# Gate/up and down products of a two-layer trunk in three 256-column matmuls a k-step, with weight places that vary by output tile

## The chip, the cores and the metric

The kernel runs on one core of a Trainium2 chip. The metric is device time in microseconds of one launch. An engine is named as the profile names it: PE is TensorE (matmuls), PEld its weight loads, DVE is VectorE, ACT is ScalarE, POOL is GpSimd, SP the engine that issues most transfers.

## The reference

The reference is a decoder trunk of two layers on 256 tokens of width 2048, batch 1, in float32. Layer 0 mixes tokens by block-sparse attention (with 256 tokens there is one block, so it is causal attention over 16 heads of 128). Layer 1 uses multi-head latent attention: low-rank queries and keys/values of rank 512, and a shared rotary key. Each is followed by a gated feed-forward network of width 5632:

```
def conv_glu_ffn(h, w_gate, w_up, conv_w, conv_b, w_down):
    g = h @ w_gate
    g = causal depthwise conv of width 3 (g) + conv_b
    return (jax.nn.silu(g) * (h @ w_up)) @ w_down

for i in range(2):
    h = rms_norm(x, attn_norm[i])
    x = x + (moba_attention if i == 0 else mla_attention)(h, ...)
    h = rms_norm(x, ffn_norm[i])
    x = x + conv_glu_ffn(h, ...)
```

All weights are float32 and are used once, so each is read once from memory.

## The kernel before

**Two parts for each operand.** Every float32 operand of a large product is split into a high part and a low part, both of type float32r: the high part is a copy in that type, the low part the rest. A product is the sum of three: high by high, high by low and low by high. An activation tile holds, per block of 128 features, 256 columns of high parts (one per token) and then 256 of low parts. So a matmul of the high weights with 512 columns does two of the three products at once, in the two halves of a PSUM bank of 512 float32 numbers, and a matmul of the low weights with the first 256 columns does the third.

**The weight stream.** `Stream` (L48 to L112) brings the weights in 370 units of up to 1 MB. The host lays them out in the order of their use. A unit holds four pieces of 128 x 512. `load` (L70) issues the transfer on SP, three units ahead. `split` (L92) makes the parts of a piece: a copy on ScalarE for the high part (L103) and a subtraction on VectorE for the low one (L104), up to four pieces ahead of their use; five buffers of each part exist. Where a part begins in its buffer is set by `starts(u, j)` (L155): each buffer has 576 elements for 512, so a part can begin up to 64 elements in. Before the change, `starts` gives the feed-forward units and the latent query rank place 0, and multiples of 8 elements elsewhere: by group of four units in the query/key/value projections of layer 0 (`HEAD_STARTS`), by pair of output tiles in the two output projections (0, 8, ... 56), and by unit in the latent stage (`LATENT_STARTS`).

**The order of the work** is written out by hand. A quantum is one piece's matmuls; `at(q, f)` puts a step behind quantum q, `first` ahead of it. The loop at the end splits the parts ahead, issues the matmuls of the quantum, and then what hangs behind it, each on its engine's own queue.

**Three forms of matmul quanta.**
- `tok_major` (L236) has the tokens in the rows of the result. Its moving operand is the weights, 512 columns at a time (288 in one projection), three products for each of two token blocks (L246, L247, L248).
- `feat_major` (L250) has the features in the rows. Its stationary operand is a 128 x 128 square of the weights, and the pair described above is issued for each square: L272 with 512 columns, L274 with 256. It serves gate/up and down of both layers and the latent query rank.
- `feat_half` (L279) issues three products of 256 columns for each square, all into one half of a bank: high by high (L286), high by low (L287), low by high (L288). It serves the two output projections, and the last output tile of the last layer's down projection.

In `feat_major` and `feat_half` a piece holds four squares, which are four steps of the contraction for one output tile of 128 features. Gate and up have 44 output tiles each, with 16 such steps (one unit) a tile; down has 16 output tiles of 44 steps (11 pieces).

**Taking results out.** After a pair, the two halves of the bank must be summed. `halves` (L290) copies the second half with ScalarE into a tile (L293), adds a base if there is one (L295), and adds the first half with VectorE (L297). `evac_gate` (L711) uses it and then scales by the norm's factor; the causal conv, SiLU and scaling follow, one step a quantum. `product` (L735) uses it for the up projection and multiplies the gate by it; `high` and `low` then make the two parts of the activation tile `a`. `residual_halves` (L384) adds a down projection's output tile to the residual stream `xT`. `cq_part` uses it for the latent query rank. Four PSUM banks are there for accumulators.

**Stages of the span.** Query/key/value of layer 0 run up to about 303 us, its output projection to 399, gate/up to 888, down to 1132; the latent attention follows to 1292, its output projection to 1400, gate/up of layer 1 to 1889, and down to the end.

Of the kernel before, what the change touches and what calls it, by code (L numbers as in the profile page):

```python
# [14 lines left out]
ALU = mybir.AluOpType  # L15
PSUM = bass.MemoryType.PSUM

P = 128
S = 256
D = 2048  # L20
NT = S // P
KD = D // P
H = 16
DFF = 5632
NF = DFF // P
# [18 lines left out]
AHEAD_PIECES = 4  # L44
WO_OPEN = 8

UP_ORDER = ("pairs", "pairs")
DOWN_ORDER = ("pairs", "pairs")  # L48

ROOM = 64  # L50

HEAD_STARTS = (2, 1, 3, 2, 1, 3, 4, 5, 6, 7, 0, 2)
LATENT_STARTS = (1, 2, 3, 4, 5, 6, 7, 2, 2, 1, 1, 3, 3)

H_START = 8

# [58 lines left out]
def trunk(ctx: ExitStack, tc: tile.TileContext, a, out):  # L115
    nc = tc.nc
# [10 lines left out]
    mm = nc.tensor.matmul  # L127
# [26 lines left out]
    units += units_of("ffn_down1")  # L154
    def starts(u, j):  # L155

        step = 0
        if u < 48:
            step = HEAD_STARTS[u // 4]
        elif u < 64 or 222 <= u < 238:  # L160
            step = (u - 48) // 2 % 8 if u < 64 else (u - 222) // 2
        elif u == 200:
            step = 2
        elif 201 <= u < 209:
            step = u - 201
        elif 209 <= u < 222:
            step = LATENT_STARTS[u - 209]
        return 8 * step, 8 * step

    assert len(units) == 370  # L170
    ws = Stream(nc, raw_pool, part_pool, units, starts)


    att = ExitStack()
    att_pool = att.enter_context(tc.tile_pool(name="att", bufs=2))
    xT = keep.tile([P, KD, S], F32, name="xT")
# [49 lines left out]
    def at(q, f, *args):  # L226
        side.setdefault(q, []).append((f, args))

    def first(q, f, *args):
        ahead.setdefault(q, []).append((f, args))  # L230

    def add(f, *args):
        quanta.append((f, args))
        return len(quanta) - 1
# [12 lines left out]
            mm(o, hi, t_lo[:, :n], start=False, stop=False)  # L247
            mm(o, lo, t_hi[:, :n], start=False, stop=kt == k_last)  # L248

    def feat_major(state, rhs, k0, k_last, t_hi, t_lo, n, order="pairs"):  # L250

        if k0 == 0:
            state["acc"] = ps_acc.tile([P, 512], F32, name="acc")
        src, o = rhs(), state["acc"]
        ks = range(n // P)
        steps = {
            "pairs": [(k, part) for k in ks for part in "hl"],  # L260
            "low first": [(k, part) for k in ks for part in "lh"],
            "grouped": [(k, part) for part in "hl" for k in ks],
        }[order]
        for i, (k, part) in enumerate(steps):
            kt = k0 + k
            flags = dict(
                start=k0 == 0 and i == 0, stop=kt == k_last and i == len(steps) - 1,
                skip_group_check=True,
            )
            c = slice(k * P, (k + 1) * P)  # L270
            if part == "h":
                mm(o, t_hi[:, c], src[:, kt, :], **flags)  # L272
            else:
                mm(o[:, :S], t_lo[:, c], src[:, kt, :S], **flags)  # L274

    def open_half(state):
        state["acc"] = ps_acc.tile([P, 512], F32, name="acc")
# [1 line left out]
    def feat_half(state, rhs, k0, k_last, first, t_hi, t_lo, n, half):  # L279

        src = rhs()
        o = state["acc"][:, half * S : (half + 1) * S]
        for k in range(n // P):
            kt = k0 + k
            w_hi, w_lo = t_hi[:, k * P : (k + 1) * P], t_lo[:, k * P : (k + 1) * P]
            mm(o, w_hi, src[:, kt, :S], start=first and k == 0, stop=False, skip_group_check=True)  # L286
            mm(o, w_hi, src[:, kt, S:], start=False, stop=False, skip_group_check=True)  # L287
            mm(o, w_lo, src[:, kt, :S], start=False, stop=kt == k_last, skip_group_check=True)  # L288

    def halves(dst, acc, base=None):  # L290

        t = small.tile([P, S], F32, name="half", bufs=2)
        nc.scalar.copy(t, acc[:, S:])  # L293
        if base is not None:
            nc.vector.tensor_tensor(t, t, base, op=ALU.add)  # L295
        dst = t if dst is None else dst
        nc.vector.tensor_tensor(dst, acc[:, :S], t, op=ALU.add)  # L297
        return dst
# [82 lines left out]
            xT[:, j, :], xT[:, j, :], state["acc"][:, half * S : (half + 1) * S], op=ALU.add  # L381
        )

    def residual_halves(state, j):  # L384
        halves(xT[:, j, :], state["acc"], xT[:, j, :])

    def store(j):
        nc.sync.dma_start(out[:, j, :], xT[:, j, :])
# [227 lines left out]
    for g in range(4):  # L616
        for kind in "qkv":
            state = {}
            for kt in range(KD):
                q = add(tok_major, state, lambda: n1.h, kt, KD - 1)  # L620
# [67 lines left out]
    ffn = {}  # L688
# [13 lines left out]
    class FTile:  # L702
# [7 lines left out]

        def evac_gate(self):  # L711
            self.g = ffn["g"][self.j % 2]
            halves(self.g[:, 2:], self.gate["acc"])
            nc.vector.tensor_tensor(self.g[:, 2:], self.g[:, 2:], self.norm.rstd_b, op=ALU.mult)

        def conv_last(self):
            self.c = ffn["pool"].tile([P, S], F32, name="c")
# [15 lines left out]
            nc.vector.tensor_tensor(self.c, self.c, self.norm.rstd_b, op=ALU.mult)  # L733

        def product(self):  # L735
            u = halves(None, self.up["acc"])
            nc.vector.tensor_tensor(self.c, self.c, u, op=ALU.mult)

        def high(self):
# [8 lines left out]
    def plan_gate_up(layer, norm):  # L748
        for j in range(NF):
            f = FTile(layer, j, norm)  # L750
            for kind, st in (("g", f.gate), ("u", f.up)):
                for kq in range(4):
                    q = add(lambda t_hi, t_lo, n, st=st, kq=kq: feat_major(
                        st, lambda: norm.h, 4 * kq, KD - 1, t_hi, t_lo, n, UP_ORDER[layer]))
                if kind == "g":
                    if j == 0:
                        at(q, open_ffn, layer)
                    at(q, f.evac_gate)
                    at(q + 1, f.conv_last)
                    at(q + 2, f.conv_rest)  # L760
                    at(q + 3, f.silu)
                    at(q + 4, f.scaled)
                else:
                    at(q, f.product)
                    at(q + 1, f.high)
                    at(q + 2, f.low)

    plan_gate_up(0, n2)

    n3 = Norm(C_AN + KD, False)  # L770

    def plan_down_feat(norm, layer):
        for j in range(KD):
            st = {}
            tail = norm is None and j == KD - 1
            if tail:
                first(len(quanta), open_half, st)
            for kq in range(NF // 4):
                if tail:
                    q = add(lambda t_hi, t_lo, n, st=st, kq=kq: feat_half(  # L780
                        st, lambda: ffn["a"], 4 * kq, NF - 1, kq == 0, t_hi, t_lo, n, 0))
                else:
                    q = add(lambda t_hi, t_lo, n, st=st, kq=kq: feat_major(
                        st, lambda: ffn["a"], 4 * kq, NF - 1, t_hi, t_lo, n, DOWN_ORDER[layer]))
            if tail:
                at(q, residual, st, j, 0)
            else:
                at(q, residual_halves, st, j)
            if norm is None:
                at(q, store, j)  # L790
            elif j < KD - 1:
                norm.plan(q + 2, j)
            else:
                at(q, norm.now, j)
                at(q + 3, norm.sums)
        return q

    plan_down_feat(n3, 0)


# [116 lines left out]
    for r in range(4):  # L917
        state = {}
        for kq in range(4):
            q = add(lambda t_hi, t_lo, n, st=state, kq=kq: feat_major(  # L920
                st, lambda: n3.h, 4 * kq, KD - 1, t_hi, t_lo, n))
            if r == 0 and kq == 0:
                at(q, open_mla)
        at(q, cq_part, state, r)
# [45 lines left out]
    for half in range(2):  # L970
        state = {}
        for kt in range(KD):
            q = add(tok_major, state, lambda: n3.h, kt, KD - 1)
# [22 lines left out]
    for g in range(4):  # L996
        if g == 1:
            rotary_queries(1, 2)
        for kind in "kqv" if g else "qkv":
            state = {}  # L1000
            for kt in range(4):
                q = add(tok_major, state, lambda kind=kind: env["cqT" if kind == "q" else "ckvT"], kt, 3)
# [18 lines left out]
    n4 = Norm(C_FN + KD, True)  # L1021
    plan_wo(n4, WO_ORDER2)
    plan_gate_up(1, n4)

    plan_down_feat(None, 1)


# [122 lines left out]
```

## Time and profile before

| | us |
|---|---|
| two runs | 2138.54 and 2138.88, median 2138.71 |
| the profiled execution | 2138.94 |
| its span, first to last instruction | 2137.1 |
| gate/up of layer 0, layer 1 | 399 to 888, 1400 to 1889 |
| down of layer 0, layer 1 | 888 to 1132, 1889 to the end |

A row of a group gives its line, engine, operation, the tile written and those read, the shape and the count; behind the first bar the busy time and the mean duration in ns of one; behind the second the engine's idle time just before it and what ended it. A row of a window gives, after its bounds, its length, and for PE, PEld, DVE, ACT and POOL the busy time and the count of instructions, then the granted clock as a share of full speed, the share of the transfer engines that was busy, and GB/s. Matmuls overlap in the rows, because the next one streams in while the last one drains, so the pace is read from starts or from counts over a window, not from durations. A row of the timeline gives the start in us and the duration.

### The profile page before, as it was taken

To read this page: it belongs to the slowest core of one execution; us is meant where nothing else is said; L and a number is where in the kernel's file an instruction comes from. 1 tells how busy PE (TensorE), PEld (TensorE's weight loads), DVE (VectorE), ACT (ScalarE), POOL (GpSimd) and SP (SyncE) were. 2 spreads that over 40 slices of the span, in tenths; PEclk is the share of its full clock that TensorE was granted. 3 is DMA by queue.
4 is the path that set the end of the run, shared out by engine and by line. 5 is a ranking of instruction groups with operands and counts; after the bars stand their busy time and mean duration, and the time that the engine had idled before them with its cause. 6 is when DMAs were issued, how large, how long until landed. Compare 5 with 4: busy or idle time off the path is not lost.

```text
span 2137.1 us, 33882 instructions
## 1 busy us (share of the span) xinstructions
PE 2129.4 (100%) x12439; PEld 1883.5 (88%) x12439; DVE 1461.7 (68%) x3246; ACT 1184.6 (55%) x2418; POOL 45.6 (2%) x37
## 2 busy tenths in 40 slices
PE   9999999999999999999999999999999999999999
PEld 7888889988888888888889889998888888888888
DVE  6766666777777777755556786777777777765554
ACT  6555555555555555545455675555555555554443
POOL 0000000000000000000000110000000000000000
PEclk9999999999999999999999999999999999999999
DMA  7444445455555555555554433555555555555553
GB/s 268 160 175 178 158 158 191 176 186 197 184 191 196 182 194 192 187 195 185 198 188 156 177 132 119 178 178 197 182 193 194 182 196 189 186 202 205 189 203 129
DMA packets 59350, 391.30 MB, mean 183 GB/s; under 512 B 6960, under 2 KB 10032, under 8 KB 13232
## 3 DMA queue, kind: packets, MB, share of 16 engines
q1 hardware_dynamic: 59040, 389.10, 51.6%
q8 instruction: 98, 1.61, 0.3%
q14 instruction: 68, 0.56, 0.1%
q10 hardware_dynamic: 144, 0.04, 0.0%
HBM read 387.01 MB, written 2.10 MB: 182 GB/s over the span
## 4 chain that ended last, share of the span: by engine, by line
PE 97%; DVE 1%; DMA 0%; issue 0%; ACT 0%; POOL 0%; SPq 0%; POOLq 0%; ACTq 0%; DVEq 0%
PE acc L272 45%; PE acc L274 24%; PE acc L247 5%; PE acc L248 5%; PE acc L246 5%; PE acc L286 3%; PE acc L288 3%; PE acc L287 3%; PE sc L511 1%; PE tp L487 1%; PE sc L558 1%; PE tp L547 0%; PE sc L514 0%; DVE wlo L104 0%; PE sc L559 0%; DMA xT<-in_xT 0%
## 5 line engine op out<-in xcount | busy, mean ns | idle before, releaser
L104 DVE TENSOR_TENSOR wlo<-raw,whi 128x512 fp32r<-128x512 f32 (+1 forms) x1480 | 991.1, 683 | 385.9 <-ACT whi L103 382.5
L103 ACT CAST whi<-raw 128x512 fp32r<-128x512 f32 (+1 forms) x1480 | 866.4, 614 | 280.3 <-PE acc L272 173.9
L272 PE MATMUL acc<-h,whi 128*128 128x512 f32 x2880 | 999.2, 390 | 0.0
L274 PE MATMUL acc<-h,wlo 128*128 128x256 f32 x2880 | 812.1, 282 | 0.0
L272 PEld LDWEIGHTS acc<-h,whi 128*128 128x128 f32 x2880 | 540.6, 188 | 113.1
L274 PEld LDWEIGHTS acc<-h,wlo 128*128 128x128 f32 x2880 | 544.3, 189 | 0.0
L272 PE MATMUL acc<-a,whi 128*128 128x512 f32 x1364 | 472.9, 390 | 0.0
L274 PE MATMUL acc<-a,wlo 128*128 128x256 f32 x1364 | 384.6, 282 | 0.0
L272 PEld LDWEIGHTS acc<-a,whi 128*128 128x128 f32 x1364 | 256.0, 188 | 53.7
L274 PEld LDWEIGHTS acc<-a,wlo 128*128 128x128 f32 x1364 | 257.8, 189 | 0.0
L293 ACT COPY half<-acc 128x256 f32<-128x256 f32 x211 | 78.7, 373 | 308.3 <-PE acc L274 308.1
L246 PE MATMUL acc<-whi,h 128*128 128x512 f32 (+1 forms) x448 | 177.1, 395 | 0.0
L247 PE MATMUL acc<-wlo,h 128*128 128x512 f32 (+1 forms) x448 | 171.0, 382 | 0.5 <-DVE wlo L104 0.5
L248 PE MATMUL acc<-whi,h 128*128 128x512 f32 (+1 forms) x448 | 170.1, 380 | 0.0
L286 PE MATMUL acc<-oT,whi 128*128 128x256 f32 x512 | 146.9, 287 | 0.0
L288 PE MATMUL acc<-oT,wlo 128*128 128x256 f32 x512 | 143.8, 281 | 0.0
L287 PE MATMUL acc<-oT,whi 128*128 128x256 f32 x512 | 143.7, 281 | 0.0
L297 DVE TENSOR_TENSOR g<-acc,half 128x256 f32<-128x256 f32 x88 | 37.4, 425 | 121.1 <-ACT half L293 121.1
L247 PEld LDWEIGHTS acc<-wlo,h 128*128 128x128 f32 x448 | 84.4, 188 | 17.2 <-DVE wlo L104 2.1
L248 PEld LDWEIGHTS acc<-whi,h 128*128 128x128 f32 x448 | 84.3, 188 | 16.8
L246 PEld LDWEIGHTS acc<-whi,h 128*128 128x128 f32 x448 | 84.4, 188 | 15.7 <-ACT whi L103 1.2
L286 PEld LDWEIGHTS acc<-oT,whi 128*128 128x128 f32 x512 | 96.7, 189 | 0.2
(153 smaller groups left out, 1594.1 us busy)
## 6 DMA issues: line engine op xcount, KB each, us to landing
raw<-in_ffn_gu SPq DMA_DIRECT2D x176, 1024.0 KB, 4.8
raw<-in_ffn_down SPq DMA_DIRECT2D x88, 1024.0 KB, 4.8
raw<-in_moba_wk SPq DMA_DIRECT2D x16, 1024.0 KB, 4.8
raw<-in_moba_wv SPq DMA_DIRECT2D x16, 1024.0 KB, 4.8
raw<-in_moba_wo SPq DMA_DIRECT2D x16, 1024.0 KB, 4.8
raw<-in_mla_wo SPq DMA_DIRECT2D x16, 1024.0 KB, 4.8
raw<-in_moba_wq SPq DMA_DIRECT2D x13, 1024.0 KB, 4.8
raw<-in_mla_wkv_a SPq DMA_DIRECT2D x8, 576.0 KB, 3.8
```

What stands on the lines that cost most here:

```text
L103: self.nc.scalar.copy(hi[:, :n], w)
L104: self.nc.vector.tensor_tensor(lo[:, :n], w, hi[:, :n].bitcast(F32), op=ALU.subtract)
L246: mm(o, hi, t_hi[:, :n], start=kt == 0, stop=False)
L247: mm(o, hi, t_lo[:, :n], start=False, stop=False)
L248: mm(o, lo, t_hi[:, :n], start=False, stop=kt == k_last)
L272: mm(o, t_hi[:, c], src[:, kt, :], **flags)
L274: mm(o[:, :S], t_lo[:, c], src[:, kt, :S], **flags)
L286: mm(o, w_hi, src[:, kt, :S], start=first and k == 0, stop=False, skip_group_check=True)
L287: mm(o, w_hi, src[:, kt, S:], start=False, stop=False, skip_group_check=True)
L288: mm(o, w_lo, src[:, kt, :S], start=False, stop=kt == k_last, skip_group_check=True)
L293: nc.scalar.copy(t, acc[:, S:])
L297: nc.vector.tensor_tensor(dst, acc[:, :S], t, op=ALU.add)
```

## The change

Three things change.

- `feat_major` takes a form instead of an order: "pair" is the two matmuls of before; "three" issues three of 256 columns in the order high by high, high by low, low by high; "between" issues the same three as high by high, low by high, high by low. All three go into the first half of the bank. Gate/up of layer 0 takes "three", gate/up of layer 1 "between", down of layer 0 "three", down of layer 1 "pair".
- With the two new forms there is nothing to sum: `halves` gives the half of the bank itself, or adds the base to it with one VectorE instruction. `evac_gate`, `product` and `residual_halves` follow.
- `starts` counts in 4 elements (16 bytes) instead of 8. In gate/up the place runs through 0 to 15 by output tile (gate tiles get the even ones, up tiles the odd ones), in down through 0 to 15 by output tile, where the last layer's low part is 8 places off the high part. The output projections take the odd places, by pair of tiles. The lists for the query/key/value groups and the latent units are new; the latent key/value rank takes place 0.

```
-UP_ORDER = ("pairs", "pairs")
-DOWN_ORDER = ("pairs", "pairs")
+FORMS = {
+    "pair": ("hb", "lh"),
+    "three": ("hh", "hl", "lh"),
+    "between": ("hh", "lh", "hl"),
+}
+UP_FORM = ("three", "between")
+DOWN_FORM = ("three", "pair")
...
-HEAD_STARTS = (2, 1, 3, 2, 1, 3, 4, 5, 6, 7, 0, 2)
-LATENT_STARTS = (1, 2, 3, 4, 5, 6, 7, 2, 2, 1, 1, 3, 3)
+HEAD_STARTS = (3, 13, 15, 1, 5, 7, 2, 2, 2, 1, 1, 13)
+LATENT_STARTS = (3, 1, 3, 5, 7, 9, 11, 13, 15, 2, 2, 6, 6, 6)
...
     def starts(u, j):
...
+        b = 0
         if u < 48:
-            step = HEAD_STARTS[u // 4]
...
+            b = HEAD_STARTS[u // 4]
+        elif u < 64:
+            b = (u - 48) // 2 * 2 + 1
+        elif u < 152:
+            b = (u - 64) % 16
+        elif u < 196:
+            b = (4 * (u - 152) + j) // 11
+        elif u == 200 or 209 <= u < 222:
+            b = LATENT_STARTS[max(u - 208, 0)]
+        elif 222 <= u < 238:
+            b = (u - 222) // 2 * 2 + 1
+        elif 238 <= u < 326:
+            b = (u - 238) % 16
+        elif u >= 326:
+            b = (4 * (u - 326) + j) // 11
+            return 4 * b, 4 * ((b + 8) % 16)
+        return 4 * b, 4 * b
...
+        tokens = {"b": slice(0, 2 * S), "h": slice(0, S), "l": slice(S, 2 * S)}
+        steps = [(k, w, t) for k in range(n // P) for w, t in FORMS[form]]
+        for i, (k, w, t) in enumerate(steps):
             kt = k0 + k
...
+            mm(
+                o if t == "b" else o[:, :S], (t_hi if w == "h" else t_lo)[:, k * P : (k + 1) * P],
+                src[:, kt, tokens[t]], start=k0 == 0 and i == 0,
+                stop=kt == k_last and i == len(steps) - 1, skip_group_check=True,
+            )
...
-    def halves(dst, acc, base=None):
-
+    def halves(dst, acc, base=None, form="pair"):
+
+        if form != "pair":
+            if base is None:
+                return acc[:, :S]
+            nc.vector.tensor_tensor(dst, acc[:, :S], base, op=ALU.add)
+            return dst
...
-            halves(self.g[:, 2:], self.gate["acc"])
-            nc.vector.tensor_tensor(self.g[:, 2:], self.g[:, 2:], self.norm.rstd_b, op=ALU.mult)
+            src = halves(self.g[:, 2:], self.gate["acc"], form=UP_FORM[self.layer])
+            nc.vector.tensor_tensor(self.g[:, 2:], src, self.norm.rstd_b, op=ALU.mult)
```

More of the change, by code (lines that the diff above doesn't have):

```diff
@@ L155, in starts @@
     def starts(u, j):
-        step = 0
+        b = 0
         if u < 48:
-            step = HEAD_STARTS[u // 4]
[L160 to L168, printed above, removed]
+            b = HEAD_STARTS[u // 4]
[15 more added lines that the diff above has]
+        return 4 * b, 4 * b
     assert len(units) == 370
@@ L248, in tok_major, with feat_major @@
             mm(o, lo, t_hi[:, :n], start=False, stop=kt == k_last)
-    def feat_major(state, rhs, k0, k_last, t_hi, t_lo, n, order="pairs"):
+    def feat_major(state, rhs, k0, k_last, t_hi, t_lo, n, form="pair"):
         if k0 == 0:
@@ L257, in feat_major @@
         src, o = rhs(), state["acc"]
[L258 to L264, printed above, removed]
+        tokens = {"b": slice(0, 2 * S), "h": slice(0, S), "l": slice(S, 2 * S)}
+        steps = [(k, w, t) for k in range(n // P) for w, t in FORMS[form]]
+        for i, (k, w, t) in enumerate(steps):
             kt = k0 + k
-            flags = dict(
-                start=k0 == 0 and i == 0, stop=kt == k_last and i == len(steps) - 1,
-                skip_group_check=True,
-            )
[L270 to L274, printed above, removed]
+            mm(
+                o if t == "b" else o[:, :S], (t_hi if w == "h" else t_lo)[:, k * P : (k + 1) * P],
+                src[:, kt, tokens[t]], start=k0 == 0 and i == 0,
+                stop=kt == k_last and i == len(steps) - 1, skip_group_check=True,
+            )
     def open_half(state):
@@ L382, in residual, with residual_halves @@
         )
-    def residual_halves(state, j):
-        halves(xT[:, j, :], state["acc"], xT[:, j, :])
+    def residual_halves(state, j, form):
+        halves(xT[:, j, :], state["acc"], xT[:, j, :], form)
     def store(j):
@@ L735, in product @@
         def product(self):
-            u = halves(None, self.up["acc"])
+            u = halves(None, self.up["acc"], form=UP_FORM[self.layer])
             nc.vector.tensor_tensor(self.c, self.c, u, op=ALU.mult)
@@ L753, in plan_gate_up @@
                     q = add(lambda t_hi, t_lo, n, st=st, kq=kq: feat_major(
-                        st, lambda: norm.h, 4 * kq, KD - 1, t_hi, t_lo, n, UP_ORDER[layer]))
+                        st, lambda: norm.h, 4 * kq, KD - 1, t_hi, t_lo, n, UP_FORM[layer]))
                 if kind == "g":
@@ L783, in plan_down_feat @@
                     q = add(lambda t_hi, t_lo, n, st=st, kq=kq: feat_major(
-                        st, lambda: ffn["a"], 4 * kq, NF - 1, t_hi, t_lo, n, DOWN_ORDER[layer]))
+                        st, lambda: ffn["a"], 4 * kq, NF - 1, t_hi, t_lo, n, DOWN_FORM[layer]))
             if tail:
@@ L787, in plan_down_feat @@
             else:
-                at(q, residual_halves, st, j)
+                at(q, residual_halves, st, j, DOWN_FORM[layer])
             if norm is None:
```

## The prediction, on record before the changed kernel ran

> **What bounds the kernel now.** I read the page's top first (engine totals, slices, chain of waits), then its costliest groups, then the table by windows of the five stages that matter, then single rows of the timeline.
>
> ```profile
> span 2137.1 us, 33882 instructions
> ...
> PE 2129.4 (100%) x12439; PEld 1883.5 (88%) x12439; DVE 1461.7 (68%) x3246; ACT 1184.6 (55%) x2418; POOL 45.6 (2%) x37
> ...
> PEclk9999999999999999999999999999999999999999
> ...
> PE 97%; DVE 1%; DMA 0%; issue 0%; ACT 0%; POOL 0%; SPq 0%; POOLq 0%; ACTq 0%; DVEq 0%
> PE acc L272 45%; PE acc L274 24%; PE acc L247 5%; PE acc L248 5%; PE acc L246 5%; PE acc L286 3%; PE acc L288 3%; PE acc L287 3%; PE sc L511 1%; PE tp L487 1%; PE sc L558 1%; PE tp L547 0%; PE sc L514 0%; DVE wlo L104 0%; PE sc L559 0%; DMA xT<-in_xT 0%
> ```
>
> TensorE is busy for the whole span at full granted clock and carries 97% of the chain; 69% of it is the pair of products (L272, 512 columns, and L274, 256 columns), most of which the change replaces. So only the pace of matmuls can move the time. Busy shares don't give that pace, because neighbouring matmul rows overlap (L272's mean is 390 ns, L274's 282, yet both fit in 347). The pace is a stage's length over its number of matmuls. In the next table the first number after the window is its length, and the next pair is TensorE's busy time and its matmuls; 331 to 399 and 1344 to 1400 are the two output projections, which already run three 256-column products (L286 to L288).
>
> ```profile
> 331.00:399.00 68.00, 68.00 (x576) 68.00 (x575) 45.77 (x88) 38.81 (x75) 0.00 (x0) 1.00 0.53 186
> 400.00:888.00 488.00, 488.00 (x2819) 432.53 (x2818) 362.90 (x708) 280.51 (x576) 1.07 (x1) 1.00 0.54 189
> 889.00:1132.00 243.00, 243.00 (x1404) 215.43 (x1403) 141.49 (x238) 121.69 (x222) 0.00 (x0) 1.00 0.54 191
> 1344.00:1400.00 56.00, 56.00 (x477) 56.00 (x476) 40.65 (x81) 33.43 (x67) 0.00 (x0) 1.00 0.54 189
> 1401.00:1888.00 487.00, 487.00 (x2813) 431.61 (x2813) 362.28 (x707) 279.55 (x575) 1.07 (x1) 1.00 0.54 189
> ```
>
> ```profile
> L272 PE MATMUL acc<-h,whi 128*128 128x512 f32 x1407 | 488.1, 390 | 0.0
> L274 PE MATMUL acc<-h,wlo 128*128 128x256 f32 x1406 | 396.5, 282 | 0.0
> ...
> L104 DVE TENSOR_TENSOR wlo<-raw,whi 128x512 fp32r<-128x512 f32 x352 | 238.3, 688 | 59.7 <-ACT whi L103 59.7
> ```
>
> The second fence is from the groups of the window 400 to 888 alone (gate/up of layer 0). Call one contraction step of 128 rows with all its products a k-step. A pair takes 488/1407 = 346.8 ns there, 243/702 = 346.2 ns in down of layer 0 (1404/2 k-steps) and 487/1406 = 346.4 ns in gate/up of layer 1: I use 346.5. Three products take 68/192 = 354.2 ns (576/3 k-steps) and 56/159 = 352.2 ns in the output projections; over both, 124/351 = 353.3 ns. Both forms stream 768 columns a k-step. Weight loads (third pair) equal the matmuls in number in both, so a second product on the same weights does not save its load (575 loads beside 576 matmuls).
>
> **The places.** The output projections move the weight parts' start by 8 elements every two output tiles (`starts`), and these rows show that this changes the pace. They are the first and last L286 of the two tiles at place 24 elements, of the two at place 32 (both in layer 1's output projection), and of the last output tile (tile `a`, place 0).
>
> ```profile
> 1344.52 0.28 PE L286 MATMUL acc<-oT,whi 128*128 128x256 f32 x1
> ...
> 1353.70 0.28 PE L286 MATMUL acc<-oT,whi 128*128 128x256 f32 x1
> ...
> 1355.47 0.28 PE L286 MATMUL acc<-oT,whi 128*128 128x256 f32 x1
> ...
> 1364.83 0.28 PE L286 MATMUL acc<-oT,whi 128*128 128x256 f32 x1
> ...
> 2118.18 0.28 PE L286 MATMUL acc<-a,whi 128*128 128x256 f32 x1
> ...
> 2130.08 0.28 PE L286 MATMUL acc<-a,whi 128*128 128x256 f32 x1
> ```
>
> Between the first two lie 27 k-steps: 9.18/27 = 340.0 ns, 113.3 a product. Between the next two, 26: 9.36/26 = 360.0 ns, 120 a product. Between the last two, 34: 11.90/34 = 350.0 ns. Same instructions, same shapes, same clock: three products cost 340 to 360 ns by place alone, and a pair at place 0 (346.5) lies inside that band. TensorE is never idle in any of these windows, so it is the products themselves that stretch.
>
> **The change part by part.**
>
> 1. Pair to three. Gate/up of each layer has 44 tiles x 2 x 16 = 1408 k-steps, down of layer 0 has 16 x 44 = 704; together 3520. The place now runs through all 16 multiples of 4 elements, tile by tile, so a mean over places is what counts, not a best one. Half the new places (the even multiples) are those of the output projections; I give them their mean, 353.3. The other half (odd multiples of 4 elements) occur nowhere in this profile: bounds 340.0 and 360.0. I take 353.3 for them too, because the rows of eight places spread over that band around this mean and nothing in them favours an end. The cost is 3520 x (353.3 - 346.5) = **+23.9 us**. Layer 1's order (high-high, low-high, high-low) has the same three products in another order; no row separates the order, so it gets the same price and the same bounds.
>
> 2. Evacuation. The ScalarE copy and one VectorE sum per tile go (176 gate/up tiles and 16 of down).
>
> ```profile
> ACT half L293 <- PE acc L274: 308.1, 207, 2.3
> DVE g L297 <- ACT half L293: 121.1, 88, 1.7
> ```
>
> ```profile
> L293 ACT COPY half<-acc 128x256 f32<-128x256 f32 x211 | 78.7, 373 | 308.3 <-PE acc L274 308.1
> ```
>
> The first two are rows of the waits (total us, times, longest), the third is from the costliest groups. I cost the removal at nothing: no matmul waits for either, TensorE being full in every window above. The wait for the tile's end moves from ScalarE to VectorE, and behind it in VectorE's queue stands the next split of weights (L104, 688 ns). ScalarE's wait is at most 2.3 us; the parts run four pieces ahead, 4 x 4 x 346.5 ns = 5.5 us, so the split still comes in time. In window 400 to 888 VectorE is busy 362.9 of 488 us and loses 88 operations, so it has more room than before. If the cover failed, the price would be up to 2.3 us a tile; nothing here suggests it.
>
> 3. Places in the first projections. Three of twelve groups (query, key, value of head group 2) move to 8 elements, the place of the first key group. First and last L246 of a stretch in the first key group and in a group that moves there:
>
> ```profile
> 32.08 0.39 PE L246 MATMUL acc<-whi,h 128*128 128x512 f32 x1
> ...
> 45.00 0.39 PE L246 MATMUL acc<-whi,h 128*128 128x512 f32 x1
> ...
> 181.01 0.40 PE L246 MATMUL acc<-whi,h 128*128 128x512 f32 x1
> ...
> 190.11 0.39 PE L246 MATMUL acc<-whi,h 128*128 128x512 f32 x1
> ```
>
> 57 products between the first two: 12.92/57 = 226.7 ns. 39 between the others: 9.10/39 = 233.3 ns. 3 groups x 16 pieces x 6 products x 6.6 ns = **-1.9 us**. The other nine groups go to odd places, between the same two paces; taken as zero. The short latent stage, whose places also change, I leave at zero as well.
>
> 4. Both output projections go to odd places: 512 k-steps, from 353.3 to between 340 and 360, -6.8 to +3.4 us; taken as zero. Down of layer 1 keeps pairs (15 tiles x 44 = 660 k-steps) but gets 16 places, with the low part 32 elements off. No row has a pair off place 0; by the band of the three products it costs 340 to 360, so -4.3 to +8.9 us; taken as zero, nearest to the pairs' own row.
>
> Sum: the profiled execution took 2138.94 us (span 2137.1 and 1.8 us around it), 0.2 us over the runs' median of 2138.71. 2138.9 + 23.9 - 1.9 = **2161 us**, +1.0%.
>
> **A rule weighed.** The page "TensorE: Matmul & The Clock Gate" of the Trainium skill (Part 2, Step-by-step, step 1) says that TensorE reads moving data and weights through two independent ports, so that "Loading the next tile's weights doesn't steal SBUF read bandwidth from the running matmul". By that the place could not matter. The trace disagrees: 340.0 against 360.0 ns with only the place of the parts changed. The same page's warm gap (section "Wait — 56ns, not 53.3ns?"), N/2.4 + 2.5 ns, would give a pair 325.0 and three products 327.5 ns, an estimate of +2.5 ns a k-step or +8.8 us (2148); the pair's 346.5 shows that it leaves out something here.
>
> **The rivals.**
> - *Place doesn't matter; only the extra product does.* Then every three costs what the last tile shows, 350.0: 3520 x 3.5 = +12.3, 2151 us. For it: that row is the only one of this form on the very tile `a` that down uses. Against it: the two rows on places. The page's two ports stand behind this one.
> - *Odd places run at the fast end.* Weights and moving data would then not meet. Odd places 340.0, even 353.3, mean 346.65: +0.5 us on the 3520; with -1.9, and -6.8 in the output projections, 2131 us, within 2% still. For it: 340.0 is a pace that holds for whole tiles without a break. Against it: only one place of eight shows it for these products.
> - *Odd places run beyond 360 (slower than before by over 2%).* A product reading weights that start off a multiple of 8 elements would stretch by one more step of the size that separates 113.3 from 120, to 126.7, or 380 a k-step. Mean of odd and even 366.7: 3520 x 20.2 = +71.1; output projections 512 x 26.7 = +13.7; 2222 us. It passes 2181.7 from a mean of 359.2 (2138.9 - 1.9 + 3520 x 12.7), that is from 365.1 at odd places, 121.7 a product. For it: no row has an odd place. Against it: 120.0 looks like a ceiling, flat for 26 k-steps.
> - That the change doesn't take hold, the second product on the same weights being free of its load, is excluded by the equal counts of loads and matmuls.
>
> **How the numbers follow.** Forecast, a mean near 353 at all places: 0.60, 2161. Place without effect: 0.10, 2151. Fast odd places: 0.19, 2131. Beyond the ceiling: 0.11, 2222. The predicted time is the first's. The first's own range is 2144 to 2178 (odd places 345 to 358, down of layer 1 in its bounds). For 8 in 10 I go from 2130, the fast case, to 2182: odd places at 360.0 give mean 356.65, 3520 x 10.15 = +35.7, plus +3.4 and up to +5 of down of layer 1's +8.9, less 1.9. Only the last rival and the far corners are left out. Faster by over 2%, about what a measurement of this kernel can tell from no change, would take 3520 k-steps at under 335 ns, below every row: 0.01. Slower by over 2%: 0.11. Within: 0.88.
>
> **What would show it.** In the profile after, window lengths over matmul counts: gate/up of both layers near 497 us instead of 488 and down of layer 0 near 248 instead of 243, with 3 matmuls a k-step. Tiles in gate/up should differ among themselves, from 340 to 360 ns a k-step by place, and with the same place again after 16 units. The L293 rows should fall from 211 to 19, TensorE's idle stay zero, and VectorE's wait for TensorE appear without a matmul waiting for L104. If every tile paces alike, the places are not the cause; if odd tiles leave the band, the ceiling is wrong; if TensorE turns idle at tile ends, the cover of step 2 failed.

## The result and the profile after

The changed kernel takes 2168.39 us (median of 2167.72 and 2169.06) against 2138.71: ratio 1.0139, 95% interval [1.0095, 1.0182]. The forecast was 2161 within 2130 to 2182, no difference beyond 2%. The profiled execution took 2167.72 us, with a span of 2165.9, which is 28.8 us over the span of before.

The top of the page after answers to the first lines shown of before:

```profile
span 2165.9 us, 40463 instructions
...
PE 2157.5 (100%) x15959; PEld 2048.4 (95%) x15959; DVE 1397.0 (64%) x3054; ACT 1150.9 (53%) x2226; POOL 45.6 (2%) x37
...
PEclk9999999999999999999999999999999999999999
...
PE 98%; DVE 1%; DMA 0%; POOL 0%; issue 0%; ACT 0%; POOLq 0%; ACTq 0%
```

There are 3520 more matmuls, as many more weight loads, and less work on VectorE and ScalarE. The chain stays TensorE's. So the time again comes from the pace of matmuls. The windows of the three changed stages and of the last down, in the same columns as in the prediction:

```profile
400.00:898.00 498.00, 498.00 (x4223) 497.90 (x4222) 334.20 (x622) 263.90 (x490) 1.07 (x1) 1.00 0.53 186
900.00:1147.00 247.00, 247.00 (x2095) 247.00 (x2094) 135.57 (x221) 120.03 (x205) 0.00 (x0) 1.00 0.53 188
1417.00:1915.00 498.00, 498.00 (x4223) 497.90 (x4222) 334.24 (x622) 266.06 (x490) 1.07 (x1) 1.00 0.53 187
1916.00:2145.00 229.00, 229.00 (x1310) 200.37 (x1309) 122.49 (x195) 103.04 (x179) 0.00 (x0) 1.00 0.56 197
```

Gate/up of layer 0 runs at 498/(4223/3) = 353.8 ns a k-step, down at 247/(2095/3) = 353.7, gate/up of layer 1 (the other order of the products) at 353.8. The last down, with pairs at 16 places, runs at 229/(1310/2) = 349.6, where it had 346.2. In three of the four stages weight loads now fill the window (the pair of numbers behind TensorE's); before, they filled 89% of it.

By stage, from the first matmul of each to the first of the next: gate/up +10.2 us in either layer, down of layer 0 +5.3, the last down +2.4, layer 1's output projection +0.4, the query/key/value groups -0.3, the latent units -0.2, layer 0's output projection -0.1; the first matmul came 0.7 us later. That is 28.8 us, all of the difference.

The tiles differ as the prediction said they would. These are the first rows of a unit at place 6 and of the unit behind it, and of a unit at place 11 and the one behind it, all in gate/up of layer 0:

```profile
434.41 0.28 PE L272 MATMUL acc<-h,whi 128*128 128x256 f32 x1
...
439.86 0.28 PE L272 MATMUL acc<-h,whi 128*128 128x256 f32 x1
...
462.70 0.28 PE L272 MATMUL acc<-h,whi 128*128 128x256 f32 x1
...
468.46 0.29 PE L272 MATMUL acc<-h,whi 128*128 128x256 f32 x1
```

A unit is 16 k-steps: 5.45/16 = 340.6 ns at place 6 (with the passage between units) and 5.76/16 = 360.0 at place 11. Read in this way for each piece, from its first product to the first of the next, with the median over the pieces of a place, three products cost by place, in ns a k-step:

| place (4 elements each) | 0 | 1 | 2 | 3 | 4 | 5 | 6 | 7 | 8 | 9 | 10 | 11 | 12 | 13 | 14 | 15 |
|---|---|---|---|---|---|---|---|---|---|---|---|---|---|---|---|---|
| gate/up, moving h | 350 | 360 | 360 | 355 | 355 | 353 | 340 | 356 | 357 | 360 | 355 | 360 | 360 | 354 | 340 | 350 |
| down, moving a | 350 | 353 | 360 | 355 | 355 | 353 | 340 | 356 | 352 | 360 | 357 | 360 | 360 | 355 | 353 | 350 |

### The profile page after: what moved, and what is told of

The parts are those of the page before. It is cut to its first block, busy times and chain, and to the rows that moved or that the text cites. A ratio compares the mean times of both kernels' runs of the same rounds, so it can differ in the third digit from the quotient of the medians.

```text
span 2165.9 us, 40463 instructions
## 1 busy us (share of the span) xinstructions
PE 2157.5 (100%) x15959; PEld 2048.4 (95%) x15959; DVE 1397.0 (64%) x3054; ACT 1150.9 (53%) x2226; POOL 45.6 (2%) x37
## 4 chain that ended last, share of the span: by engine, by line
PE 98%; DVE 1%; DMA 0%; POOL 0%; issue 0%; ACT 0%; POOLq 0%; ACTq 0%
PE acc L272 69%; PE acc L259 5%; PE acc L260 5%; PE acc L258 5%; PE acc L290 3%; PE acc L289 3%; PE acc L288 3%; PE sc L518 1%; PE tp L494 1%; PE sc L565 1%; PE sc L521 0%; PE tp L554 0%; PE sc L566 0%; DVE wlo L109 0%; DMA xT<-in_xT 0%; POOL hr L437 0%
## 5 line engine op out<-in xcount | busy, mean ns | idle before, releaser
L108 ACT CAST whi<-raw 128x512 fp32r<-128x512 f32 (+1 forms) x1480 | 883.2, 614 | 471.3 <-PE acc L272 344.9
L272 PE MATMUL acc<-h,whi 128*128 128x256 f32 x5696 | 1020.1, 282 | 0.0
L272 PEld LDWEIGHTS acc<-h,whi 128*128 128x128 f32 x5696 | 875.4, 189 | 2.4
L272 PE MATMUL acc<-a,whi 128*128 128x256 f32 (+1 forms) x2068 | 480.5, 317 | 0.0
L272 PEld LDWEIGHTS acc<-a,whi 128*128 128x128 f32 x2068 | 340.1, 188 | 28.8
L721 DVE TENSOR_TENSOR g<-acc,rstd_b 128x256 f32<-128x256 f32 x88 | 37.4, 425 | 129.8 <-PE acc L272 126.8
L726 ACT ACTIVATE c<-g,par 128x256 f32<-128x256 f32 x88 | 53.1, 603 | 107.4 <-DVE g L721 107.4
```

What stands on the lines that cost most here:

```text
L108: self.nc.scalar.copy(hi[:, :n], w)
L272: mm(o if t == "b" else o[:, :S], (t_hi if w == "h" else t_lo)[:, k * P : (k + 1) * P], src[:, kt, tokens[t]], start=k0 == 0 and i == 0, s ...
L721: nc.vector.tensor_tensor(self.g[:, 2:], src, self.norm.rstd_b, op=ALU.mult)
L726: nc.scalar.activation(self.c, self.g[:, 2:], AF.Identity, bias=par[:, cb : cb + 1], scale=self.cw(2))
```

## The experiments

Unless said otherwise, the lines below are of the experiments' own profiles. Spans are compared with 2137.1 us before and 2165.9 after.

### The form alone

The changed kernel, with `starts` and its two lists as they were before, so that gate/up and down have place 0:

```diff
-HEAD_STARTS = (3, 13, 15, 1, 5, 7, 2, 2, 2, 1, 1, 13)
-LATENT_STARTS = (3, 1, 3, 5, 7, 9, 11, 13, 15, 2, 2, 6, 6, 6)
+HEAD_STARTS = (2, 1, 3, 2, 1, 3, 4, 5, 6, 7, 0, 2)
+LATENT_STARTS = (1, 2, 3, 4, 5, 6, 7, 2, 2, 1, 1, 3, 3)
...
-        return 4 * b, 4 * b
+        return 8 * step, 8 * step
```

> The three products of the change with all the places of before (gate/up and down at place 0). Theory (the pace of each product is set by the place of the weight parts; the change costs the mean over 16 places): place 0 runs at the 350.0 ns a k-step of the tiles at place 0 in the profile after, against 346.7 for the pair, so 3520 x 3.3 = +11.6 us, span near 2149, ratio 1.005. Rival (the third product costs about 7 ns a k-step wherever the parts lie): the whole +24 to +26 us of the three stages stays, span near 2162, ratio 1.011.

Span 2149.2 us, ratio to before 1.0057 [1.0040, 1.0073].

```profile
400.00:893.00 493.00, 493.00 (x4227) 1.00 0.53 188
```

493/(4227/3) = 349.9 ns, the same in every piece, where the rival wanted 353.8. The form alone costs 12.1 us; the third product has no fixed price.

### The places alone

```diff
-UP_FORM = ("three", "between")
-DOWN_FORM = ("three", "pair")
+UP_FORM = ("pair", "pair")
+DOWN_FORM = ("pair", "pair")
```

> The changed places with the pair kept in every stage. Theory (place sets the pace of pairs too): the tiles of gate/up and down run at 346.5 to 353.5 ns by place as the pairs of the last down do in the profile after, mean 350.2, so 3520 x 3.5 = +12.3 and +2.4 in the last down: span near 2152, ratio 1.007. Rival (the place matters only for three products, since a 512-column product hides the conflict): gate/up and down of layer 0 at 346.7 for every tile, span near 2139 with the last down's +2.4, ratio 1.001.

Span 2151.3 us, ratio 1.0065 [1.0050, 1.0080].

```profile
400.00:892.00 492.00, 492.00 (x2815) 1.00 0.54 187
893.00:1139.00 246.00, 246.00 (x1408) 1.00 0.54 189
```

492/(2815/2) = 349.6 ns and 246/704 = 349.4. By piece, pairs cost 346.8 at places 0, 2 to 5 and 8, and up to 353.8 at others; no median is under that. So pairs feel the place too, and before they stood at their best. The places alone cost 14.2 us, of which 2.4 in the last down. Form and places each explain about half: 12.1 + 14.2 = 26.3 of 28.8. They don't simply add, because the two forms like different places: in gate/up three products take 340 and a pair 353 at place 6, but 360 and 347 at place 2.

### One place throughout

```diff
         elif u < 152:
-            b = (u - 64) % 16
+            b = 6
         elif u < 196:
-            b = (4 * (u - 152) + j) // 11
+            b = 6
...
         elif 238 <= u < 326:
-            b = (u - 238) % 16
+            b = 6
```

> The changed kernel with place 6 (24 elements) for every tile of gate/up of both layers and down of layer 0. Theory (place sets the pace, and holds from tile to tile): 340.0 ns a k-step in all three stages, 3520 x (340.0 - 354.1) = -49.6 us on the changed kernel's 2165.9: span near 2116, ratio to before 0.990, with the last down still +2.4. Rival (the fast pace at place 6 is a passing state that needs the place of the tile ahead to differ; in the output projection of layer 0 before, place 24 elements ran at 353): 353 ns or more in down of layer 0 or everywhere, span 2126 to 2163.

Here the theory failed, and the times lie where its rival had them. The profiled span is 2163.1 us, and ten executions fell on two times, five at 2164.9 to 2165.5 us and five at 2136.8 to 2137.9; in the order of the list they alternate without exception. The start of gate/up of layer 0 shows how (rows of the low-by-high product, first of a stretch and last):

```profile
399.86 0.28 PE L272 MATMUL acc<-h,wlo 128*128 128x256 f32 x1
...
403.26 0.28 PE L272 MATMUL acc<-h,wlo 128*128 128x256 f32 x1
...
403.72 0.50 PE L368 MATMUL tp<-ones,nacc 128*128 128x1 f32 x4
...
404.40 0.28 PE L272 MATMUL acc<-h,wlo 128*128 128x256 f32 x1
...
405.08 0.28 PE L272 MATMUL acc<-h,wlo 128*128 128x256 f32 x1
...
405.62 0.43 PE L378 MATMUL tp<-ident,rstd 128*128 128x128 f32 x2
...
406.48 0.28 PE L272 MATMUL acc<-h,wlo 128*128 128x256 f32 x1
...
417.79 0.28 PE L272 MATMUL acc<-h,wlo 128*128 128x256 f32 x1
```

Ten k-steps at 3.40/10 = 340 ns; then the norm puts six small matmuls of its own between. The first four (L368) leave the pace at 0.68/2 = 340 ns; behind the last two (L378) come 32 k-steps at 11.31/32 = 353.4 ns, with nothing else changed. It stays so to the end of the stage and through down:

```profile
410.00:890.00 480.00, 480.00 (x4078) 1.00 0.52 187
898.00:1146.00 248.00, 248.00 (x2108) 1.00 0.53 187
```

480/(4078/3) = 353.1 and 248/(2108/3) = 352.9 ns. So place 6 has two steady paces, and a disturbance can pass the stream from one to the other. It doesn't always: in the profiles of this and the later runs, gate/up meets these six matmuls at place 6 fourteen times, and five times the stream is at 353 ns behind them (both layers here, layer 1 in three later runs), nine times still at 340. The 27.7 us between the executions' two groups is what 347 pieces of gate/up and 176 of down at 13.3 ns a k-step make (4 x 13.3 x 523 = 27.8), so in the shorter executions one layer's gate/up and the first down most likely kept 340 ns; this is worked out and not shown, since no trace is of a shorter one.

### The moving operand shifted

```diff
-H_START = 8
+H_START = 16
```

> The changed kernel with the activation tile h moved by 8 elements (H_START 16 instead of 8), a unchanged. Theory (what counts is the place of the weight parts against the place of the moving operand): in gate/up the whole table by place shifts by two, so the fast places are 8 and 0 instead of 6 and 14, and in down of layer 0 (moving operand a) it stays; total within 5 us of the changed kernel, since the mean over 16 places is the same. Rival (the place of the parts by itself counts): places 6 and 14 stay at 340.0 ns in gate/up.

Span 2168.5 us, ratio 1.0147 [1.0132, 1.0162]. First rows of the units at place 6 and place 8 in gate/up of layer 0, and of those behind them:

```profile
435.94 0.28 PE L272 MATMUL acc<-h,whi 128*128 128x256 f32 x1
...
441.62 0.28 PE L272 MATMUL acc<-h,whi 128*128 128x256 f32 x1
...
447.27 0.28 PE L272 MATMUL acc<-h,whi 128*128 128x256 f32 x1
...
452.72 0.28 PE L272 MATMUL acc<-h,whi 128*128 128x256 f32 x1
```

Place 6 now takes 5.68/16 = 355.0 ns and place 8 5.45/16 = 340.6. The median row of gate/up moves by two places almost number for number (340 at 8 and 0, 350 at 1 and 2, 360 at 3, 4, 11, 13 and 14), while the row of down, whose moving tile `a` was not shifted, has its 340 at place 6 as before; of down's row, only place 1 moved (353 to 360), which the shift doesn't explain. What counts is the place of the weights against that of the moving operand.

### A change of place now and then

In gate/up of both layers and down of layer 0, against the kernel with place 6 throughout:

```diff
-            b = 6
+            b = 5 if u % 8 == 2 else 6
```

> Place 6 as in the run with place 6 alone, but place 5 in every eighth unit of the three stages, so that the place changes now and then. Theory (a place allows several paces; the pace at hand stays until something disturbs it, and a change of place from 5 to 6 sets the fast one): units at place 6 run at 340.0 ns a k-step, those at 5 at 353.3, mean 341.7: gate/up 481 us each instead of 499, down of layer 0 240.5 instead of 249.4, span near 2121, and no scatter of 28 us between executions. Rival (which pace is taken is chance at the start of an execution): executions still differ by 10 to 28 us, spans between 2120 and 2163.

Span 2122.8 us, ratio 0.9970 [0.9940, 1.0001], since three of ten executions took 2148.2 to 2148.8 and seven 2122.8 to 2123.5.

```profile
400.00:880.00 480.00, 480.00 (x4216) 1.00 0.54 193
882.00:1121.00 239.00, 239.00 (x2100) 1.00 0.55 194
```

341.6 and 341.4 ns in the profiled one. In gate/up of layer 1 the norm's matmuls again left the stream at 353 ns. The next unit at place 5 ended that; these are the last low products of that unit and of the first two pieces at place 6 behind it:

```profile
1418.53 0.28 PE L272 MATMUL acc<-h,wlo 128*128 128x256 f32 x1
...
1419.91 0.28 PE L272 MATMUL acc<-h,wlo 128*128 128x256 f32 x1
...
1421.27 0.28 PE L272 MATMUL acc<-h,wlo 128*128 128x256 f32 x1
```

Four k-steps at 1.38/4 = 345 ns, the next four at 1.36/4 = 340. So a change of place does set the lower pace, in this trace. It isn't a passing state either, as the rival of the run with one place had it: the seven units between two such changes keep 340 ns. That no scatter would be left was wrong.

The same with another place in every eighth unit:

> As the run with every eighth unit at place 5, with 7 in its stead. If any change of place into 6 sets the fast pace: span near 2123 (place 7 runs at 356.3, so 0.9 us more than with 5), with the same scatter of 26 us in some executions. If it is the place before that decides: all units at 6 stay at 353.3, gate/up 498, down 249, span near 2165.

> As the run with every eighth unit at place 5, with 0 in its stead, from which place 6 is never entered in any run so far. If any change of place into 6 sets the fast pace: span near 2122. If the place before decides: span near 2162.

Spans 2124.5 us with place 7, ratio 0.9943 [0.9928, 0.9958], and 2122.3 with place 0, ratio 0.9929 [0.9912, 0.9945]. Place 6 ran at 340 ns behind either, so it isn't the place before that decides. With place 0, too, the norm left gate/up of layer 1 at 353 ns, and the next change of place ended that. Their four executions each lay within 2 us. These runs still don't show that 7 or 0 is safer: with three long executions in ten, at random, four in a row without one come about in one case of four, and those three don't even look random (they are the second, fifth and eighth on the list). These two runs were also on another chip than the run with place 5.

### The summed-up version

```diff
-UP_FORM = ("three", "between")
-DOWN_FORM = ("three", "pair")
+UP_FORM = ("three", "three")
+DOWN_FORM = ("three", "three")
...
+        b = 2
+        if 48 <= u < 64 or 222 <= u < 238:
+            b = 5 if u % 4 == 0 else 6
+        elif 196 <= u < 200:
+            b = 0
+        elif 64 <= u < 196 or u >= 238:
+            b = 5 if u % 8 == 2 else 6
         return 4 * b, 4 * b
```

> Three products everywhere, places 6 and 5 as in the run with every eighth unit at 5, also in the last down and (every fourth unit at 5) in both output projections, and place 2 in the query/key/value groups of layer 0 and the latent units. By the same theory: from the changed kernel's span of 2165.9, gate/up -18 each, down -9 and -6, output projections -3 each, query/key/value -4, latent -1: about 2104, ratio to before 0.985. Rival (chance): scatter between executions, 2104 to 2150.

Span 2109.0 us, ratio 0.9912 [0.9875, 0.9950]. Eight executions: five at 2109.1 to 2110.9 us, three at 2133.6 to 2134.4; all lie below the kernel before. The last two rows are of the profile before.

```profile
6.00:301.00 295.00, 293.18 (x1359) 1.00 0.52 188
302.00:394.00 92.00, 92.00 (x797) 1.00 0.51 184
395.00:876.00 481.00, 481.00 (x4225) 1.00 0.54 193
877.00:1116.00 239.00, 239.00 (x2100) 1.00 0.54 194
...
6.00:303.00 297.00, 296.23 (x1359) 1.00 0.53 186
304.00:399.00 95.00, 95.00 (x797) 1.00 0.50 178
```

The gain is where it was expected: gate/up at 481/(4225/3) = 341.5 ns; the same number of matmuls as before in 295 instead of 297 us in the query/key/value groups and in 92 instead of 95 in the output projection. It is 5 us short of the 2104 expected, of which 2 us in the query/key/value groups and 2 us in the two gate/up stages.

The run with place 5 and the summed-up version ran once more, for the trace of a longer execution:

> The run with every eighth unit at place 5, once more, for the trace of another execution. Three of ten executions took 26 us more. If this one is such: theory (the entries into place 6 went to the slow pace in gate/up and down of one layer, 16 + 8 us), whole stages at 353.3 ns a k-step at place 6; rival (the extra lies elsewhere, a wait or a transfer): stages at 340 and a gap of TensorE. If it is not: span 2123 and the same rows.

> The fastest version once more, for the trace of another execution, read as the run before: span 2108 or 2132, and in the second case which stages run at 353.3 ns a k-step at place 6.

Spans 2123.8 and 2107.2 us: neither was one. Which stages lose the 24 to 26 us stays open.

### The evacuation

On the kernel with the form alone, the copy is put back in gate/up (down, which adds its sum with a base, is left as it was):

```diff
             if base is None:
-                return acc[:, :S]
+                t = small.tile([P, S], F32, name="half", bufs=2)
+                nc.scalar.copy(t, acc[:, :S])
+                return t
```

> The run with three products and all places of before, with one ScalarE copy (128 x 256) a gate/up tile put back between the bank and VectorE. Theory (evacuation lies beside the matmuls): span 2149.2 as without it, within 0.5 us. Rival (the shorter evacuation gave something back): up to 176 x 0.37 = 65 us more.

Span 2149.8 us against 2149.2. In one execution of each, gate/up takes what it took without the copies, to 0.01 us (493.62 in either layer, from first matmul to first matmul), and the 0.6 us lie in the query/key/value groups, which have no such copy.

```profile
L290 ACT COPY half<-acc 128x256 f32<-128x256 f32 x176 | 66.0, 375 | 275.6 <-PE acc L265 275.6
```

66 us of ScalarE work cost nothing.

### Fewer columns, the same loads

On the kernel with the form alone:

```diff
+            r = tokens[t]
+            if form != "pair" and w + t != "hh":
+                r = slice(r.start, r.start + P)
             mm(
-                o if t == "b" else o[:, :S], (t_hi if w == "h" else t_lo)[:, k * P : (k + 1) * P],
-                src[:, kt, tokens[t]], start=k0 == 0 and i == 0,
+                o if t == "b" else o[:, : r.stop - r.start],
+                (t_hi if w == "h" else t_lo)[:, k * P : (k + 1) * P],
+                src[:, kt, r], start=k0 == 0 and i == 0,
```

> The run with three products and all places of before, but the two small products (high-low, low-high) of gate/up and of the first down take only the first 128 of 256 tokens, so that part of the correction is left out. If a product costs at least the pace of its weight load (the 128-column transposes run at 110 ns each), a k-step takes 116.7 + 2 x 110 = 337 ns: 3520 x 13 = -47, span near 2102. If the streamed columns set the pace, 116.7 + 2 x 58 = 233 ns, until VectorE with its splits becomes the bound: span under 1900.

Span 2117.3 us, in one execution; the kernel leaves out half of the two small products. A third of the columns is gone from every k-step (512 instead of 768), and

```profile
881.00:1119.00 238.00, 238.00 (x2103) 1.00 0.55 195
```

it still takes 238/(2103/3) = 339.5 ns, 113.2 for each of its three loads. The trace points at the loads and not at the columns: in down the starts of the products lie 169, 58 and 112 ns apart, those of the loads, nearly evenly, 120, 108 and 112.

```profile
999.81 0.19 PEld L268 LDWEIGHTS acc<-a,whi 128*128 128x128 f32 x1
999.93 0.19 PEld L268 LDWEIGHTS acc<-a,wlo 128*128 128x128 f32 x1
1000.04 0.30 PEld L268 LDWEIGHTS acc<-a,whi 128*128 128x128 f32 x2
1000.27 0.19 PEld L268 LDWEIGHTS acc<-a,wlo 128*128 128x128 f32 x1
```

So a product of three doesn't get below its load, and at 340 ns the full three products are already there. Their columns may hold them at the same pace: a 512-column product of the first projections took 226.7 ns at best, twice 113.3. These runs don't tell the two apart. The expected span of 2102 assumed 110 a load and 116.7 for the long product.

## Why the prediction was right, step by step

*What bounds.* TensorE's pace; no window after has a gap.

*Step 1, pair to three.* +23.9 us was forecast, 25.8 came. The size of the step was the difference of 353.3 and 346.5; the stages ran at 353.8. The even places came out at 352.1 in gate/up (mean of the table's row), the odd ones, which no row of before had, at 356.0: nearer to the upper end of the bounds, and not over it by more than 0.3 (medians). So the guess for the odd places was 2.7 ns low and the price of the even ones 1.2 high; that the two errors partly cancel is luck. The order of the products made no difference, as priced. The reason, that the mean over places counts, is shown by the form alone at place 0: 349.9 ns and 12.1 us.

*Step 2, evacuation at nothing.* Right, and shown by the kept copy for gate/up. VectorE's wait for the tile's end, as a row of the waits after has it, and the copies that are left:

```profile
DVE g L721 <- PE acc L272: 126.8, 86, 1.6
```

```profile
L300 ACT COPY half<-acc 128x256 f32<-128x256 f32 x19 | 7.1, 373 | 42.5 <-PE acc L272 42.5
```

At most 1.6 us, with 5.5 us of parts ahead; no row of TensorE's own waits names a matmul of the three stages.

*Step 3, -1.9 us in the first projections.* It came to -0.3. The three groups did gain, 1.5 us (two of them ran at 227 ns a product throughout), but the groups at odd places, taken as zero, gave most of it back: the two key groups that had been at the best place, 226.7 ns, went to places at about 233 and lost 1.0.

*Step 4, taken as zero within -11.1 and +12.3 us.* The output projections came to +0.3 together. The last down, mis-sized at zero, cost +2.4: the reason given (nearest to the pairs' own row) didn't allow for place 0 being one of the best places of a pair, which a row at a single place can't tell. These misses, with the 0.7 us later start, make up the 7 us between forecast and profiled execution. Two bounds don't come out of the prediction's own terms: odd places at 345 with the last down at its low end give 2142, not 2144, and the terms named for 2182 add up to 2181. Neither touches the forecast.

*The rivals.* Place without effect is refuted by the table and by the run with one place shifted. The two independent ports of the Trainium skill's page "TensorE: Matmul & The Clock Gate" (Part 2, Step-by-step, step 1) would make the shift of h by 8 elements harmless, and place 8 went from 357 to 341 ns by it: the trace disagrees. Fast odd places: no median was under 350. Beyond the ceiling: none was over 360.5.

*What the prediction had wrong beneath a right number.* It took the pace as a function of place ("by place alone"). The profile before already spoke against that. These are two L286 rows of the tiles at place 24 elements (place 6 in the new count) in layer 0's output projection, 27 k-steps apart:

```profile
343.43 0.28 PE L286 MATMUL acc<-oT,whi 128*128 128x256 f32 x1
...
352.96 0.28 PE L286 MATMUL acc<-oT,whi 128*128 128x256 f32 x1
```

9.53/27 = 353.0 ns, where the prediction's rows of the same place in layer 1's have 340.0. (After the change the two projections agree place by place, so it isn't that `oT` lies elsewhere.) The run with one place showed it for long streams: a place only allows certain paces, and what went before picks one. That the mean came right all the same is most likely because the places change with every unit, and in the same order; in gate/up, pieces at one place agree within 3 ns from the third unit on. No run has the 16 places in another order, so this reason is argued.

## What to carry to other kernels

Read the pace of back-to-back matmuls from a window's length over its count, and compare stages that differ in one thing: here a stage of before that already had the new form gave the price within 2 us. Where weights are used for only 256 columns, the load is about as long as the product (113 ns against 113 to 120 here), and the place of the weights against the moving tile is worth up to 6%: sweep it by output tile, then take the best, but time several executions, since the pace can depend on what ran before.

## What the runs showed of the hardware

- A load of a 128 x 128 float32r square takes 113.2 ns in a stream (339.5/3 with fewer columns). The Trainium skill's page "TensorE: Matmul & The Clock Gate", section "LDWEIGHTS (loading the stationary operand)", gives columns/1.2, an estimate of 106.7 ns for 128; the stream here is 6% slower.
- Three products a k-step run between 340 and 360 ns by the place of the weights against the moving operand, in steps of 16 bytes with a period of 256 (under the shift by two places the two ends of the table join: 14 went to 0, 15 to 1); pairs between 346.8 and 353.8.
- At the same place, the same stream holds 340 ns (28 pieces on end, 38 us) or 353 (hundreds of us); six foreign matmuls passed it from 340 to 353 in five of fourteen passages, a change of place passed it back in the three traces that have one behind such a passage. What made three executions in ten 26 us longer (three in eight 24 us) in spite of such changes was not found.
